# A macaron encoder block on one core: second-half FFN operands summed from PSUM, three pairs of products up front, filler transposes, and a new order in the mixer

## The chip, the cores and the metric

The kernel runs on one core of one Trainium2 chip. The metric is the device time of one execution in microseconds (us). Three runs of the kernel before gave 1774.66, 1774.74 and 1776.48 us, so the median is 1774.74 us.

## The reference

The reference computes one residual layer on a sequence of 1024 tokens with 1024 features, in float32:

```
x = x + 0.5 * swiglu(rmsnorm(x), w_gate, w_up, w_down)         # FFN 1, hidden width 2816
h = rmsnorm(x) @ w_in                                          # u 512 | v 512 | c_q 256 | c_kv 128 | k_rope 32
y_a = gelu(u) * (masked w_s[g] @ rmsnorm(gelu(v)) + b[g])      # 4 groups of 128 channels, blocks of 128 tokens
y_b = attention(q(c_q), k(c_kv, k_rope), v(c_kv))              # 8 heads, rmsnorm of q and k, rope, causal by chunks of 64
x = x + concat(rmsnorm(y_a), rmsnorm(y_b)) @ w_out
x = x + 0.5 * swiglu(rmsnorm(x), ...)                          # FFN 2
x = rmsnorm(x)
```

## The kernel before

**Products in two parts.** Every float32 operand of a matmul is split into a rounded high part (a cast on ACT) and a low part (a subtraction on DVE). Each product is then three matmuls on PE: high by high, high by low, low by high. One gate/up product of the FFN is 24 matmuls of 512 columns (line 464).

**Strassen in the FFN.** Each FFN multiplies by a seven-product scheme in place of eight. For each of 11 units of weight columns, `GateUp` makes seven products P1 to P7. P1 and P2 need only the first four row tiles of x (operands B11 and B21). P6, P5, P7, P3 and P4 need sums that contain the last four row tiles (T2, T1, T3, B22, T4). `XOps` makes these operands. `XOps.tile` (line 356) normalizes one row tile, transposes it on PE into two PSUM banks and copies both banks to SBUF on ACT. After the fourth tile it splits B11 and B21 from SBUF. For each of the last four tiles, `second` (line 371) forms T3, T2 and T4 from SBUF and splits T2. `rest` (line 392) forms T1 and splits the others later. The order of products begins with P1 and P2 of units 0 and 1 (`EARLY`, line 512). The PSUM group "a" of a unit, two of the eight banks, stays open from P1 to P4.

**The mixer.** Steps run in a list written out by hand (`for ch in ...`): u_t projects the gate channels of row tile t, m and g do the spatial mixing of a pair of tiles, a_t projects the latents, c_t transposes them and splits the result into `chl` (lines 290, 291), l_t (`latent_tile`, line 887) multiplies to queries, keys and values (lines 895 to 904), normalizes them and rotates the queries on POOL (lines 794 to 798). u4 to u7 stand between the latent steps. Attention follows after l7: 32 items, each of one head and a pair of row tiles. The first four items need only row tiles 0 to 3. `head_T` transposes the queries and keys of a head, four row tiles at a time; item 3 begins with those of row tiles 4 to 7.

**What sets the order.** A `Step` holds its work and work to be issued so many steps ahead (`before`). SBUF and PSUM places are planned from a dry run in which a matmul counts as one unit of time and any other operation as 0.01. A place whose earlier tile is still in use makes the later one wait. Small tiles rotate over 6 buffers for each width (line 179). Last, a scheduler that simulates the timeline puts the instructions of each engine in order, so that the order on an engine can differ from the order in the text. Loads go through SP's queue in program order.

Of the kernel before, what the change touches and what calls it, by code (L numbers as in the profile page):

```python
# [234 lines left out]
def block(nc, x, positions, ffn1_norm, ffn1_w_gate, ffn1_w_up,  # L235
# [61 lines left out]
    def transposed(src, name):  # L297
        halves = [bank(f"tp{i}_{name}") for i in range(2)]
# [51 lines left out]
    class XOps:  # L350
# [5 lines left out]
        def tile(self, i, xt, g):  # L356
            xn = tile_([P, D], f"xn{i}_{self.nm}")
            normed(xt, g, xn, f"{self.nm}{i}")
            hv = transposed(xn, f"{self.nm}{i}")
            n, c = i // 4, (i % 4) * P  # L360
            for k in range(2):
                if i % 4 == 0:
                    self.b[k, n] = tile_([P, 4, 512], f"b{k}{n}_{self.nm}")
                nc.scalar.copy(self.b[k, n][:, :, c:c + P], hv[k])
            if i == 3:
                self.split("B11", self.b[0, 0])
                self.split("B21", self.b[1, 0])
# [28 lines left out]
        def rest_of(self, key):  # L396
            b11, b12 = self.b[0, 0], self.b[0, 1]
            if key == "T1":
                for a, b in HALVES:
                    nc.vector.tensor_tensor(b12[:, a:b], b12[:, a:b], b11[:, a:b], op=ALU.subtract)  # L400
                    self.split("T1", b12, ((a, b),))
            else:
                self.split(key, {"T3": self.t3, "B22": self.b[1, 1], "T4": self.b[1, 0]}[key])
# [9 lines left out]
    class GateUp:  # L413
# [83 lines left out]
        def steps(self, order, floor=0, loaded=(), load_at=()):  # L497
            at = {}
            for u, (pn, ka, kb, pair) in order:
                st = at[u, pn] = Step(lambda u=u, a=(pn, ka, kb, pair): self.product(u, *a))  # L500
                if pn == "P1":
                    for k in range(2):
                        if (u, k) not in loaded:
                            lead = st.index - load_at[u] if u < len(load_at) else LEAD_LOAD - k
# [4 lines left out]
                st.before(LEAD_SPLIT, lambda u=u, ka=ka: self.split(u, ka), floor)  # L509
# [139 lines left out]
    xts = [row_tile(x[rows(0), :], "xa0")]  # L649
    g1 = row_tile(ffn1_norm[0].partition_broadcast(P), "g1")  # L650
    xts += [row_tile(x[rows(t), :], f"xa{t}") for t in (1, 2, 3)]
# [291 lines left out]
    vs = [Step(lambda t=t: v_tile(t)) for t in range(NT)]  # L943
    sm = {}
    works = {"u": u_tile, "m": mix_pair, "g": gmlp_pair, "a": latent_in, "k": key_rope, "c": latent_T, "l": latent_tile}
    for ch in ("u0 u1 m0 g0 u2 u3 m1 g1 a0 c0 a1 k0 l0 u4 c1 a2 l1 c2 a3 k1 l2 u5 m2 c3 a4 l3 g2 c4 a5 k2 l4 u6 "
               "c5 a6 c6 l5 a7 c7 k3 l6 u7 m3 l7").split():
        sm[ch] = Step(lambda f=works[ch[0]], n=int(ch[1]): f(n))
    v0 = vs[0].index
    vs[0].before(12, mix_gain)  # L950
    for t in range(4):
        steps[v0 - 5 + t].do(lambda t=t: mix_norm_tile(t))
    for t in range(4, NT):
        vs[t].before(4, lambda t=t: mix_norm_tile(t), v0)
    for j in range(2):
        vs[0].before(8 - j, lambda j=j: load_in("wv", j, GW, GW))
        sm["u0"].before(7 - j, lambda j=j: load_in("wu", j, 0, GW))
        sm["a0"].before(9 - j, lambda j=j: load_in("wa", j, 2 * GW, LAT))
    for k, (lv, lu, la) in enumerate(((4, 5, 7), (3, 5, 6), (2, 4, 5), (1, 3, 4))):
        vs[0].before(lv, lambda k=k: split_in("wv", k, GW))  # L960
        sm["u0"].before(lu, lambda k=k: split_in("wu", k, GW))
        sm["a0"].before(la, lambda k=k: split_in("wa", k, LAT))
    vs[0].before(3, v_gain)
    sm["u0"].before(3, spatial_weights)
    sm["u1"].before(0, out_gain)
    sm["a0"].before(6, load_uq)
    sm["a0"].before(4, latent_setup)
    sm["a0"].before(4, load_kv)
    sm["a0"].before(1, split_uq)
    sm["a0"].before(1, split_kv)  # L970
    sm["a0"].before(0, rope_tables)
    sm["l7"].do(lambda: mx.__setitem__("yB", [tile_([P, 4, H, DV], f"yB{i}") for i in range(2)]))

# [84 lines left out]
    for n in range(len(items) + D2):  # L1058
        st = att[n] = Step()
        if n == 0:  # L1060
            st.do(lambda: head_T(0, 0))
            st.do(lambda: head_T(1, 0))
        if n == 3:
# [16 lines left out]
    att[0].do(lambda: gmlp_pair(3))  # L1080
# [64 lines left out]
    gu2.steps(GU_ORDER, base2, load_at=(base2 - 1, base2))  # L1145
# [62 lines left out]
```

## Time and profile before

| | |
|---|---|
| median of 3 runs | 1774.74 us |
| profiled execution | 1775.43 us |
| its span, first to last instruction | 1773.4 us |
| PE busy | 1714.4 us (97%) |
| DVE busy | 1123.7 us (63%) |
| ACT busy | 757.0 us (43%) |
| mean granted TensorE clock | 0.989 |

PE is TensorE's matmuls, PEld its weight loads, DVE VectorE, ACT ScalarE, POOL GpSimd, SP the queue that issues loads. The granted clock is a share of full speed: 1.00 is 2.4 GHz and 0.50 is 1.2 GHz. An idle time is put down to the instruction that ended it, with an arrow.

### The profile page before, as it was taken

To read this page: it belongs to the slowest core of one execution; us is meant where nothing else is said; L and a number is where in the kernel's file an instruction comes from. 1 tells how busy PE (TensorE), PEld (TensorE's weight loads), DVE (VectorE), ACT (ScalarE), POOL (GpSimd) and SP (SyncE) were. 2 spreads that over 40 slices of the span, in tenths; PEclk is the share of its full clock that TensorE was granted. 3 is DMA by queue.
4 is the path that set the end of the run, shared out by engine and by line. 5 is a ranking of instruction groups with operands and counts; after the bars stand their busy time and mean duration, and the time that the engine had idled before them with its cause. 6 is when DMAs were issued, how large, how long until landed. Compare 5 with 4: busy or idle time off the path is not lost.

```text
span 1773.4 us, 21088 instructions
## 1 busy us (share of the span) xinstructions
PE 1714.4 (97%) x8132; PEld 1439.8 (81%) x8132; DVE 1123.7 (63%) x1497; ACT 757.0 (43%) x1151; POOL 149.5 (8%) x287
## 2 busy tenths in 40 slices
PE   7999999999999999988799999999999999999998
PEld 5788888888888888877699888778888888888886
DVE  7966556545578666554877644684656655558774
ACT  7523333334334444444777833352333233433442
POOL 2000000000000013322300511100000000000010
PEclk9999999999999999998899999999999999999999
DMA  6323232226844521200000332424233222683531
GB/s 202 115 93 119 98 111 89 96 89 220 311 129 162 183 85 48 69 10 3 13 1 1 120 101 87 140 95 137 76 120 108 95 90 90 231 301 110 179 129 48
DMA packets 122979, 199.48 MB, mean 112 GB/s; under 512 B 11008, under 2 KB 57600, under 8 KB 122880
## 3 DMA queue, kind: packets, MB, share of 16 engines
q1 hardware_dynamic: 118784, 184.52, 30.7%
q0 software_dynamic: 3520, 12.58, 1.8%
q8 instruction: 63, 1.03, 0.2%
q10 hardware_dynamic: 576, 1.05, 0.2%
q14 instruction: 36, 0.29, 0.0%
HBM read 143.07 MB, written 55.05 MB: 112 GB/s over the span
## 4 chain that ended last, share of the span: by engine, by line
PE 89%; DVE 4%; ACT 3%; DMA 1%; POOL 1%; issue 1%; SPq 0%; POOLq 0%; ACTq 0%; DVEq 0%
PE psum L464 45%; PE psum L594 8%; PE psum L596 8%; PE psum L597 8%; PE psum L1026 2%; PE psum L722 2%; PE psum L724 2%; PE psum L723 2%; PE psum L1125 1%; PE psum L1126 1%; PE psum L1128 1%; PE psum L300 1%; PE psum L1036 1%; PE psum L1035 1%; PE psum L997 1%
## 5 line engine op out<-in xcount | busy, mean ns | idle before, releaser
L480 DVE TENSOR_TENSOR P_b<-psum,P_b 128x1024 f32<-128x1024 f32 x33 | 40.3, 1222 | 93.0 <-PE psum L464 93.0
L480 DVE TENSOR_TENSOR P_a<-psum,P_a 128x1024 f32<-128x1024 f32 x33 | 40.3, 1222 | 91.8 <-PE psum L464 91.8
L470 ACT COPY P_b<-psum 128x1024 f32<-128x1024 f32 x33 | 33.4, 1014 | 70.3 <-PE psum L464 68.3
L470 ACT COPY P_a<-psum 128x1024 f32<-128x1024 f32 x33 | 33.4, 1013 | 69.1 <-PE psum L464 69.1
L271 POOL TENSOR_TENSOR r_fin<-ms_fin,mhalf 128x1 f32<-128x1 f32 x8 | 8.0, 1009 | 609.4 <-DVE ms_fin L269 609.3
L291 DVE TENSOR_TENSOR pl<-psum,ph 128x512 fp32r<-128x512 f32 (+1 forms) x80 | 48.5, 630 | 10.8 <-ACT ph L290 10.2
L481 ACT ACTIVATE P_a<-P_a 128x512 f32<-128x512 f32 x33 | 20.8, 631 | 80.8 <-DVE P_a L480 80.7
L1001 DVE TENSOR_REDUCE nm<-psum 128x1 f32<-128x128 f32 (+3 forms) x64 | 46.8, 749 | 11.8 <-PE psum L999 11.5
L481 ACT ACTIVATE P_b<-P_b 128x512 f32<-128x512 f32 x33 | 20.8, 632 | 73.0 <-DVE P_b L480 72.9
L1125 PE MATMUL psum<-woh,yh 128*128 128x512 f32 x128 | 50.5, 396 | 0.0
L1003 ACT ACTIVATE p<-psum,nm 128x128 f32<-128x128 f32 (+3 forms) x64 | 47.7, 750 | 6.4 <-DVE nm L1001 3.4
L1126 PE MATMUL psum<-wol,yh 128*128 128x512 f32 x128 | 50.2, 392 | 0.0
L703 POOL DMA_DIRECT2D x1d<-x_a x8 | 4.6, 580 | 510.6 <-DVE x_a L608 510.5
L1026 PE MATMUL psum<-ident,p 128*128 128x128 f32 x288 | 43.4, 281 | 3.8 <-ACT p L1003 3.8
L1128 PE MATMUL psum<-woh,yl 128*128 128x512 f32 x128 | 44.9, 391 | 0.0
L290 ACT CAST ph<-psum 128x512 fp32r<-128x512 f32 (+1 forms) x80 | 41.7, 559 | 7.0 <-PE psum L1026 6.8
L1036 PE MATMUL psum<-pl,vv 128*128 128x256 f32 x160 | 42.7, 293 | 1.2 <-DVE pl L291 1.2
L1035 PE MATMUL psum<-ph,vv 128*128 128x256 f32 x160 | 43.3, 294 | 0.2 <-ACT ph L290 0.2
L997 PE MATMUL psum<-kh,qh 128*128 128x512 f32 (+2 forms) x96 | 38.6, 404 | 1.0 <-ACT kh L986 0.9
L1026 PEld LDWEIGHTS psum<-ident,p 128*128 128x128 f32 x288 | 34.0, 145 | 6.4 <-ACT p L1003 4.8
L608 DVE SCALAR_TENSOR_TENSOR x_b<-psum,x_b 128x512 f32<-128x512 f32 x32 | 21.0, 686 | 26.9 <-PE psum L597 26.9
L464 PE MATMUL psum<-xB11h_f,A11h_a 128*128 128x512 f32 x88 | 35.4, 405 | 2.6 <-ACT xB11h_f L389 2.6
(525 smaller groups left out, 5753.3 us busy)
## 6 DMA issues: line engine op xcount, KB each, us to landing
raw_a<-in_ffn_w_gate SPq DMA_DIRECT2D x22, 512.0 KB, 4.3
raw_a<-in_ffn_w_up SPq DMA_DIRECT2D x22, 512.0 KB, 5.4
hd<-hS_a SPq DMA_DIRECT2D x44, 256.0 KB, 2.2
raw_b<-in_ffn_w_gate SPq DMA_DIRECT2D x22, 512.0 KB, 4.2
raw_b<-in_ffn_w_up SPq DMA_DIRECT2D x22, 512.0 KB, 5.2
hd<-hS_b SPq DMA_DIRECT2D x44, 256.0 KB, 2.1
aS_a<-hd SPq DMA_DIRECT2D x20, 512.0 KB, 4.2
wB_a<-in_ffn_w_down SPq DMA_DIRECT2D x20, 512.0 KB, 5.6
```

Source lines behind the costliest of these rows:

```text
L464: mm(o, lhs[:, 4 * m + k, :], rhs[:, k, :], start=pn in FIRST and n == 0, stop=n == 11, skip_group_check=True)
L470: nc.scalar.copy(ev[u, pn], bk)
L480: nc.vector.tensor_tensor(c, bk, c, op=ALU.add)
L594: mm(banks[t], hh[:, j, tl], dh[:, j, :], start=pn in DOWN_FIRST and c == 0 and j == 0, stop=False, skip_group_check=True)
L596: mm(banks[t], hh[:, j, tl], dl[:, j, :], start=False, stop=False, skip_group_check=True)
L597: mm(banks[t], hl[:, j, tl], dh[:, j, :], start=False, stop=c == 5, skip_group_check=True)
L1026: nc.tensor.transpose(ps[:, i * P:(i + 1) * P], prs[j][:, c * P:(c + 1) * P], ident)
L1035: mm(acc[:, 0:256], mx["vv"][c][:, h, :], hi, start=i == 0, stop=False)
L1036: mm(acc[:, 0:256], mx["vv"][c][:, h, :], lo, start=False, stop=i == len(pts) - 1)
L1125: mm(pe[e], yh[:, k, :], wh[:, es], start=k == 0, stop=False)
L1126: mm(pe[e], yh[:, k, :], wl[:, es], start=False, stop=False)
L1128: mm(pe[e], yl[:, k, :], wh[:, e * 512:(e + 1) * 512], start=False, stop=k == KD - 1)
```

## The change

1. `XOps.tile` splits B11 and B21 of the first four row tiles straight from PSUM, tile by tile (`cut`), and copies the plain values to SBUF as well (`keep`). In FFN 1 the `keep` copies and the B21 parts come after the fourth tile.
2. `second` takes T1 and T2 from PSUM in two subtractions. The two sums for T3 and T4 move to `rest`.
3. `EARLY` has P1 and P2 of three units. The `rest` steps and one row tile move back to fit.
4. In FFN 1 the first four tiles get their eight PSUM banks by name, the second row tile is loaded before the gain, and transposes of the identity matrix are issued ahead of the first tile (40) and after tiles 0, 1 and 2 (8 each). They are written to a bank that tile 3 overwrites.
5. In FFN 2 the first weights are loaded one step earlier, three units' weights are asked for at the head, and the splits may come one step earlier.
6. The mixer's order has all u, m and g steps before the latents, and attention items 0, 1 and 2 between the last latent steps. The attention functions move up in the file unchanged.
7. Small tiles rotate over 10 buffers.

```diff
-        self.smalls = ctx.enter_context(tc.tile_pool(name="sp", bufs=6))
+        self.smalls = ctx.enter_context(tc.tile_pool(name="sp", bufs=10))
...
-        def tile(self, i, xt, g):
+        def tile(self, i, xt, g, halves=None, later=False):
             xn = tile_([P, D], f"xn{i}_{self.nm}")
             normed(xt, g, xn, f"{self.nm}{i}")
-            hv = transposed(xn, f"{self.nm}{i}")
...
-                nc.scalar.copy(self.b[k, n][:, :, c:c + P], hv[k])
-            if i == 3:
-                self.split("B11", self.b[0, 0])
-                self.split("B21", self.b[1, 0])
+            hv = transposed(xn, f"{self.nm}{i}", halves)
...
+            work = [lambda key=key, v=v, op=op: op(key, v, cs) for key, v in zip(("B11", "B21"), hv) for op in (self.cut, self.keep)]
+            work.pop(0)()
+            return work if later else [w() for w in work]
+
+        def cut(self, key, v, cs):
+            hi, lo = (o[:, :, cs] for o in self.ops[key])
+            split(v, hi, lo)
+
+        def keep(self, key, v, cs):
+            nc.scalar.copy(self.b[key][:, :, cs], v)
...
-            nc.vector.tensor_tensor(t3, b22, b12, op=ALU.subtract)
-            nc.vector.tensor_tensor(t2, t3, b11, op=ALU.add)
+            nc.vector.tensor_tensor(t1, hv[0], b11, op=ALU.subtract)
+            nc.vector.tensor_tensor(t2, hv[1], t1, op=ALU.subtract)
             self.last = (nc.scalar.copy(hi, t2), nc.vector.tensor_tensor(lo, t2, f(hi), op=ALU.subtract))
-            nc.vector.tensor_tensor(b21, b21, t2, op=ALU.subtract)
+            nc.scalar.copy(b22, hv[1])
...
+            for a, e in HALVES:
+                if key == "T3":
+                    nc.vector.tensor_tensor(b["B21"][:, a:e], b["B21"][:, a:e], b["T2"][:, a:e], op=ALU.subtract)
+                    nc.vector.tensor_tensor(b["T2"][:, a:e], b["T2"][:, a:e], b["B11"][:, a:e], op=ALU.subtract)
+                self.split(key, b[{"T3": "T2", "T4": "B21"}.get(key, key)], ((a, e),))
...
-    EARLY = [(0, BY_NAME["P1"]), (0, BY_NAME["P2"]), (1, BY_NAME["P1"]), (1, BY_NAME["P2"])]
+    EARLY = [(u, BY_NAME[p]) for u in range(3) for p in ("P1", "P2")]
...
+    def warm(count):
+
+        for _ in range(count):
+            nc.tensor.transpose(tbanks[3, 1][:, 0:P], ident, ident)
+
+    warm(40)
+    later = []
     for t in range(4):
-        xo1.tile(t, xts[t], g1)
+        later.append(xo1.tile(t, xts[t], g1, [tbanks[t, k] for k in range(2)], True))
+        if t < 3:
+            warm(8)
+        if t == 1:
+            later[0].pop(0)(), later[1].pop(0)()
+    for work in (later[2].pop(0), later[3].pop(0), *(w.pop(0) for w in later), *(w.pop(0) for w in later)):
+        work()
...
-    for i, j in ((4, 0), (5, 0), (6, 1), (7, 1)):
+    for i, j in ((4, 0), (5, 0), (6, 1), (7, 2)):
...
-        for key, j in (("T1", 2), ("T3", 3), ("B22", 3), ("T4", 4)):
+        for key, j in (("T1", 4), ("T3", 5), ("B22", 5), ("T4", 6)):
...
-    for ch in ("u0 u1 m0 g0 u2 u3 m1 g1 a0 c0 a1 k0 l0 u4 c1 a2 l1 c2 a3 k1 l2 u5 m2 c3 a4 l3 g2 c4 a5 k2 l4 u6 "
-               "c5 a6 c6 l5 a7 c7 k3 l6 u7 m3 l7").split():
+    for ch in ("u0 u1 m0 g0 u2 u3 m1 g1 u4 u5 m2 g2 u6 u7 m3 g3 a0 c0 a1 k0 l0 c1 a2 l1 c2 a3 k1 l2 c3 a4 l3 c4 a5 k2 l4 "
+               "c5 a6 c6 a7 l5 c7 k3 x0 l6 x1 l7 x2").split():
+        if ch[0] == "x":
+            attend(int(ch[1]))
+            continue
...
-    gu2.steps(GU_ORDER, base2, load_at=(base2 - 1, base2))
+    gu2.steps(GU_ORDER, base2 - 1, load_at={(0, 0): base2 - 2, (0, 1): base2 - 1, (1, 0): base2, (1, 1): base2,
+                                             (2, 0): base2, (2, 1): base2})
```

## Rows read from the trace of the kernel before

**Rows 1.** The page, its first part (busy time of each engine, share of the span, instructions) and two lines of its second (busy tenths of PE and the granted clock in 40 equal slices of 44.3 us).

```profile
PE 1714.4 (97%) x8132; PEld 1439.8 (81%) x8132; DVE 1123.7 (63%) x1497; ACT 757.0 (43%) x1151; POOL 149.5 (8%) x287
...
PE   7999999999999999988799999999999999999998
...
PEclk9999999999999999998899999999999999999999
```

**Rows 2.** Busy time in stretches: the stretch and its length, then the busy us and instructions of PE, PEld, DVE, ACT and POOL, the granted clock, the share of the DMA engines and GB/s.

```profile
0.00:60.00 60.00, 46.00 (x203) 37.04 (x204) 48.22 (x59) 44.90 (x63) 11.35 (x23) 0.94 0.47 158
626.50:738.00 111.50, 111.50 (x544) 94.32 (x543) 73.88 (x112) 46.78 (x76) 29.53 (x33) 1.00 0.23 75
738.00:872.00 134.00, 108.69 (x505) 94.69 (x504) 75.00 (x213) 69.29 (x167) 47.26 (x98) 0.90 0.03 11
872.00:1025.00 153.00, 147.79 (x1086) 137.72 (x1085) 116.71 (x229) 118.39 (x275) 32.28 (x77) 0.99 0.12 41
1117.00:1165.00 48.00, 41.76 (x192) 33.27 (x191) 35.99 (x40) 25.54 (x33) 4.24 (x4) 1.00 0.41 136
...
0.00:19.40 19.40, 7.26 (x33) 5.83 (x33) 9.55 (x13) 12.98 (x21) 3.69 (x17) 1.00 0.91 326
19.40:26.40 7.00, 6.12 (x14) 4.40 (x15) 6.56 (x7) 5.88 (x8) 2.53 (x1) 0.52 1.07 357
```

**Rows 3.** Waits in 738 to 872 us, of PE (first two) and of ACT: who waited for whom, us in total, times, the longest.

```profile
PE psum L895 <- ACT chl L290: 9.9, 5, 3.9
PE psum L902 <- ACT chl L290: 1.0, 1, 1.0
ACT chl L290 <- POOL qn L798: 14.7, 4, 5.5
```

**Rows 4.** The timeline of POOL, ACT and PE around the second latent tile: start, duration, engine, line, operation.

```profile
762.91 0.73 POOL L798 TENSOR_TENSOR qn<-rt 128x256 f32<-128x256 f32 x1
783.09 0.73 POOL L798 TENSOR_TENSOR qn<-rt 128x256 f32<-128x256 f32 x1
763.68 0.48 ACT L290 CAST chl<-psum 128x384 fp32r<-128x384 f32 x1 [0.94 <-POOL qn L798]
774.92 1.28 ACT L852 ACT_TABLE_LOAD   x1
776.84 1.28 ACT L277 ACT_TABLE_LOAD   x1
783.86 0.48 ACT L290 CAST chl<-psum 128x384 fp32r<-128x384 f32 x1 [5.51 <-POOL qn L798]
769.92 0.81 PE L904 MATMUL psum<-wkv_h,chl 128*128 128x512 f32 x2
```

**Rows 5.** Groups by line in 738 to 872 us that are not of the latents: count, busy us and mean ns, idle before.

```profile
L277 ACT ACT_TABLE_LOAD x5 | 6.4, 1283 | 0.1
L852 ACT ACT_TABLE_LOAD x4 | 5.1, 1283 | 0.1
L874 DVE SCALAR_TENSOR_TENSOR ya<-u,r_ya,goA 128x512 f32<-128x512 f32 x5 | 4.3, 853 | 0.7 <-POOL r_ya L271 0.7
L868 DVE SCALAR_TENSOR_TENSOR u<-psum,bT,u 128x256 f32<-128x256 f32 x8 | 3.6, 479 | 6.5 <-PE psum L861 5.2 <-ACT u L852 1.2
L1001 DVE TENSOR_REDUCE nm<-psum 128x1 f32<-128x128 f32 (+3 forms) x6 | 2.2, 421 | 0.0
L987 DVE SCALAR_TENSOR_TENSOR kl<-psum,gkcol,kh 128x512 fp32r<-128x512 f32 x3 | 2.2, 736 | 0.0
```

**Rows 6.** The timeline of PE in the latent projection at full clock: two matmuls that stand three apart.

```profile
755.00 0.35 PE L722 MATMUL psum<-wa_h,xmh 128*128 128x416 f32 x1
755.56 0.35 PE L722 MATMUL psum<-wa_h,xmh 128*128 128x416 f32 x1
```

**Rows 7.** The head of FFN 1: waits of PE, then the timeline.

```profile
PE psum L464 <- ACT xB11h_f L389: 2.6, 1, 2.6
PE psum L464 <- DVE xB11l_f L390: 0.9, 1, 0.9
PE psum L464 <- DVE xT1l_f L390: 1.0, 1, 1.0
7.93 1.06 ACT L286 ACTIVATE xn_f<-xa 128x1024 f32<-128x1024 f32 x1 [2.16 <-DMA xa<-in_x]
14.09 1.28 DVE L305 SCALAR_TENSOR_TENSOR xn_f<-xa,r_f,g 128x1024 f32<-128x1024 f32 x1 [0.73 <-POOL r_f L271]
16.79 1.22 DVE L435 TENSOR_TENSOR S_a<-raw_a,raw_a 128x1024 f32<-128x1024 f32 x1 [0.28 <-PE psum L300]
18.26 2.00 ACT L389 CAST xB11h_f<-b_f 128x1024 fp32r<-128x1024 f32 x2
19.37 1.22 PE L464 MATMUL psum<-xB11h_f,A11h_a 128*128 128x512 f32 x2 [2.62 <-ACT xB11h_f L389]
```

**Rows 8.** Weight loads of the row tiles' transposes in FFN 1: the first tile (8 to 11 us) and the fourth (15.4 to 17 us) as groups, and the fifth, at about 30 us, from the timeline.

```profile
L300 PEld LDWEIGHTS psum<-ident,xn_f 128*128 128x128 f32 x8 | 1.6, 224 | 8.0 <-DVE xn_f L305 8.0
L300 PEld LDWEIGHTS psum<-ident,xn_f 128*128 128x128 f32 x8 | 1.1, 172 | 0.5 <-DVE xn_f L305 0.5
30.17 1.03 PEld L300 LDWEIGHTS psum<-ident,xn_f 128*128 128x128 f32 x8
```

**Rows 9.** The head of FFN 2: waits of PE in 1117 to 1165 us, and of SP's queue in 1085 to 1140 us.

```profile
PE psum L464 <- DVE S2l_b L450: 2.2, 1, 2.2
PE psum L464 <- DVE xT1l_f L390: 2.1, 1, 2.1
PE psum L464 <- ACT b_f L364: 1.3, 1, 1.3
SPq L311 <- PE psum L1128: 34.4, 4, 20.0
```

More of the change, by code (lines that the diff above doesn't have):

```diff
@@ L295, in split_scaled, with transposed @@
         nc.vector.scalar_tensor_tensor(lo, src, scale, f(hi), op0=ALU.mult, op1=ALU.subtract)
-    def transposed(src, name):
-        halves = [bank(f"tp{i}_{name}") for i in range(2)]
+    def transposed(src, name, halves=None):
+        halves = halves or [bank(f"tp{i}_{name}") for i in range(2)]
         for k in range(KD):
@@ L371, in second @@
-        def second(self, i, cs):
-            b11, b12, b21, b22 = (v[:, :, cs] for v in (self.b[0, 0], self.b[0, 1], self.b[1, 0], self.b[1, 1]))
+            hv = transposed(xn, f"{self.nm}{i}", halves)
+            cs = slice((i % 4) * P, (i % 4) * P + P)
+            if i >= 4:
+                return self.second(i, hv, cs)
+            if i == 0:
+                for k, key in enumerate(("B11", "B21")):
+                    self.ops[key] = [tile_([P, 4, 512], f"x{key}{n}_{self.nm}", F32R) for n in "hl"]
+                    self.b[key] = tile_([P, 4, 512], f"b{k}_{self.nm}")
@@ L396, in rest_of @@
         def rest_of(self, key):
[L397 to L403, printed above, removed]
+            b = self.b
+            for a, e in HALVES:
[3 more added lines that the diff above has]
+                self.split(key, b[{"T3": "T2", "T4": "B21"}.get(key, key)], ((a, e),))
     PRODUCTS = (("P1", "A11", "B11", "a"), ("P2", "A12", "B21", "b"), ("P6", "S2", "T2", "a"), ("P5", "S1", "T1", "c"),
@@ L495, in hsum, with steps @@
             nc.vector.tensor_tensor(t, self.h[u, x0], self.h[u, x1], op=op)
-        def steps(self, order, floor=0, loaded=(), load_at=()):
+        def steps(self, order, floor=0, loaded=(), load_at={}):
             at = {}
@@ L508, in steps @@
                         st.before(LEAD_SUM - which, lambda u=u, w=which: self.sums(u, w), floor)
[L509 removed]
+                st.before(LEAD_SPLIT if len(at) != 2 else 1, lambda u=u, ka=ka: self.split(u, ka), floor)
             return at
[L512 removed]
+    EARLY = [(u, BY_NAME[p]) for u in range(3) for p in ("P1", "P2")]
     GU_ORDER = EARLY + [(u, p) for u in range(NU) for p in PRODUCTS if (u, p) not in EARLY]
@@ L648, in block @@
     gu1 = GateUp("a", xo1, ffn1_w_gate[0], ffn1_w_up[0], hds[0])
-    xts = [row_tile(x[rows(0), :], "xa0")]
+    xts = [row_tile(x[rows(t), :], f"xa{t}") for t in range(2)]
     g1 = row_tile(ffn1_norm[0].partition_broadcast(P), "g1")
-    xts += [row_tile(x[rows(t), :], f"xa{t}") for t in (1, 2, 3)]
+    xts += [row_tile(x[rows(t), :], f"xa{t}") for t in (2, 3)]
     for k in range(2):
@@ L1057, in block, with attend @@
     att = {}
-    for n in range(len(items) + D2):
+    def attend(n):
         st = att[n] = Step()
@@ L1062, in block @@
             st.do(lambda: head_T(1, 0))
+        if n == D2 - 1:
+            st.do(lambda: mx.__setitem__("yB", [tile_([P, 4, H, DV], f"yB{i}") for i in range(2)]))
         if n == 3:
@@ L1078, in block @@
                 st.do(lambda i=items[n - D1]: weighted(*i))
-    att[0].do(lambda: gmlp_pair(3))
+    vs = [Step(lambda t=t: v_tile(t)) for t in range(NT)]
+    sm = {}
+    works = {"u": u_tile, "m": mix_pair, "g": gmlp_pair, "a": latent_in, "k": key_rope, "c": latent_T, "l": latent_tile}
+    for ch in ("u0 u1 m0 g0 u2 u3 m1 g1 u4 u5 m2 g2 u6 u7 m3 g3 a0 c0 a1 k0 l0 c1 a2 l1 c2 a3 k1 l2 c3 a4 l3 c4 a5 k2 l4 "
[3 more added lines that the diff above has]
+            continue
+        sm[ch] = Step(lambda f=works[ch[0]], n=int(ch[1]): f(n))
+    v0 = vs[0].index
+    vs[0].before(12, mix_gain)
+    for t in range(4):
+        steps[v0 - 5 + t].do(lambda t=t: mix_norm_tile(t))
+    for t in range(4, NT):
+        vs[t].before(4, lambda t=t: mix_norm_tile(t), v0)
+    for j in range(2):
+        vs[0].before(8 - j, lambda j=j: load_in("wv", j, GW, GW))
+        sm["u0"].before(7 - j, lambda j=j: load_in("wu", j, 0, GW))
+        sm["a0"].before(9 - j, lambda j=j: load_in("wa", j, 2 * GW, LAT))
+    for k, (lv, lu, la) in enumerate(((4, 5, 7), (3, 5, 6), (2, 4, 5), (1, 3, 4))):
+        vs[0].before(lv, lambda k=k: split_in("wv", k, GW))
+        sm["u0"].before(lu, lambda k=k: split_in("wu", k, GW))
+        sm["a0"].before(la, lambda k=k: split_in("wa", k, LAT))
+    vs[0].before(3, v_gain)
+    sm["u0"].before(3, spatial_weights)
+    sm["u1"].before(0, out_gain)
+    sm["a0"].before(6, load_uq)
+    sm["a0"].before(4, latent_setup)
+    sm["a0"].before(4, load_kv)
+    sm["a0"].before(1, split_uq)
+    sm["a0"].before(1, split_kv)
+    sm["a0"].before(0, rope_tables)
+    for n in range(3, len(items) + D2):
+        attend(n)
     wov = w_out[0].rearrange("(k p) e -> p k e", p=P)
```

46 lines of the change are left out of this document (9 added, 37 removed).

## The prediction

> **What bounds the kernel now.** I read the page first. PE is busy 97% of the span, and its line of tenths is full but for the first slice and for slices 18 to 20, where the granted clock dips too [rows 1]. So the kernel is bound by TensorE, no matmul is removed by the change, and all that can be won is time in which PE is idle or runs at 1.2 GHz. The table of stretches says where that is [rows 2]. From 626 to 738 us, the first half of the mixer, PE has no idle time. From 738 to 872 us, the latents, it is idle 134.0 - 108.7 = 25.3 us, and the mean clock is 0.90. In the head of FFN 1 it is idle 14.0 us of 60, in the head of FFN 2 6.2 us of 48. Attention (872 to 1025) loses 5.2 us, which the change leaves alone. Then I asked what PE waited for in each: in the latents mostly for `chl`, the latents' split on ACT, and that in turn for POOL's rotation of the tile before [rows 3].
>
> **The change part by part.**
>
> *Mixer.* First what it costs now. A mean of 0.90 over 134 us means that 10%, 13.4 us, of PE's rate was not granted. Some of this fell on idle time (25.3 of 134, a fifth), so I take 11 us as lost. With the idle time the stretch has 36 us above PE's own work.
>
> Where it comes from: in the timeline POOL ends a query at 763.64 and ACT begins `chl` at 763.68; POOL ends the next at 783.82 and ACT begins at 783.86 [rows 4]. That is a buffer that has to come free (the code has no other tie between them): the dry run counts a vector operation as nothing, and at this point weights for u, the gated unit's v, and the growing queries and keys share SBUF. Each such loop empties PE for several us and its clock falls. The four u steps inside make it worse on ACT: nine table loads of 1.28 us, 11.5 us, between Gelu and Sqrt [rows 5].
>
> After the change, u4 to u7 and the last two mixing pairs are done before the latents. Their PE work is moved and not removed. The u weights and v are dead by then, which frees over 12,000 floats per partition of a plan of some 51,000 (line 210), and the nine table loads fall to about four (one Sqrt after the last Gelu, and Exp against Sqrt at the end). So I expect the buffer loop to be gone. What then bounds a latent tile? PE: three matmuls of 416 columns take 0.56 us [rows 6], so a projection of 24 takes 4.5 us; the l step has 12 matmuls of 384 and 6 of 512 columns, 7680 columns against 9984, so 3.5 us; with the transposes 8.4 us. DVE: 75.0 us in the stretch, less 7.9 for the gated unit and some 7 for attention's first items [rows 2, 5], is 60 us, 7.5 a tile. POOL and ACT are below that. PE is the slowest, but only just: I leave 3 us for places where DVE's order holds it up. The tail is worse. From the last matmul of an l step (769.92, two matmuls, so about 770.6) to the end of its rotation (783.82) it was 13.2 us, of which two table loads are 2.6 [rows 4]. With one Exp against Sqrt load I take 12 us; item 2 of attention covers some 2.5, so 9.5 us of idle time before `head_T` of tiles 4 to 7, and 2.5 us of lower clock behind it. Sum left: 3 + 9.5 + 2.5 = 15 of the 36. **Mixer: -21 us**, between -30 (the tail is covered too) and +27 (second rival).
>
> *Head of FFN 1.* The first product now starts at 19.37 [rows 7]: the fourth tile is normalized at 14.09 + 1.28, transposed, copied on ACT, then cast from SBUF, with a weight sum in front on DVE. After the change the cast reads PSUM: 15.4, plus half a tile's transposes (0.55), plus a cast of 512 columns (half of 1.0, rounded up to 0.6) gives 16.5, so -2.9. The second row tile lands 1.3 us or so earlier by the swap of loads, which gives slack ahead of the fourth tile and no more. The wait for the low part (0.9) goes, since it is made per tile. So does the wait for T1 (1.0): three pairs of 2 x 5.3 us stand ahead of P6, one pair more than now, and DVE's sums per second-half tile fall from four to three. The two that are put off into `rest`, and unit 2's splits, come to some 7 us of DVE within those 10.7. Against it, B21's casts and the `keep` copies now stand on ACT behind the fourth tile, 16 casts and copies of about 0.6 in place of 8 copies and 4 casts of 1.0: I charge 1.0 us at the start of P2.
>
> The clock: from 19.4 to 26.4 it is 0.52 [rows 2], after PE stood idle 2.6 us. At half pace 7 us do the work of 3.5, and the change can win about 3.0 of it if the filler keeps the clock up. Whether a transpose can: the first tile's eight loads took 1.6 us and the fourth's 1.1, against 1.03 for a tile at full clock [rows 8], while nothing but transposes had run. So the pace did rise on transposes alone. (The clock column reads 1.00 up to 19.4 us, also where the pace was slow; in this stretch I go by the pace.) The filler has room: 40 at 0.2 us fill 8 us from 1.9 us on, and the fourth tile's transposes are not due until 15.4. **FFN 1: -2.9 - 0.9 - 1.0 - 3.0 + 1.0 = -6.8 us**, between -8 and +2 (third rival).
>
> The Trainium skill says otherwise of the filler: its page "TensorE: Matmul & The Clock Gate", section "Part 4: PE-mode transpose", says that a transpose does not count as activity for the clock. The pace of the fourth tile speaks against it in this kernel; by the page the filler would lift nothing, which is the third rival below.
>
> *Head of FFN 2.* Idle 6.2 us: 2.2 and 2.1 on DVE (S2's and T1's low parts), the rest on weights and banks at the first products [rows 9]. The third pair takes the first two away as above. The earlier load helps only if SBUF is free then, since SP's queue stood 34.4 us waiting for the output projection's matmuls [rows 9]. I keep 2.2 of the 6.2. **FFN 2: -4 us**, between -6 and +2 (six loads of 1 MB compete in place of four).
>
> *At nothing:* the ten small buffers (they free latent tiles' scalars; counted with the buffer loop); attention's functions moved in the file; u and g steps in front, where PE is never idle and DVE is 66% busy [rows 2]. If that cover were too thin, a pair of g steps on DVE would show as waits there.
>
> **Sum.** 1775.4 (the profiled execution) - 21 - 6.8 - 4 = 1743.6. The median of the runs stands 0.7 below the profiled one, so **1743 us**.
>
> **The rivals.**
>
> 1. *The buffer loop stays in half of the tiles.* For it: the plan's clock still ignores vector work. Against: over 12,000 floats are freed. The mixer then wins about 4 us, and the sum is 1775.4 - 4 - 10.8 - 0.7 = 1760.
> 2. *Slower: the loop stays in every latent tile, with no u steps left to fill it.* A loop took 783.86 - 763.68 = 20.2 us [rows 4]; without two table loads, 17.6. PE has 8.4 us of work in it, so it idles and stays at the lower clock. Eight loops of 17 are 136 us, and the moved u and m steps cost 25 us of PE before (four u of 5.5, two pairs of 1.4): 161 in place of 134, +27. With both heads' 10.8 won: 1791 us. It decides once a loop is longer than (134 - 25 + 10.8) / 8 = 15 us.
> 3. *The filler does not lift the clock.* 64 fillers and 24 transposes ahead of the fourth tile at 0.196 us are 17.3 us from 1.9, so its transposes start at 19.2 and the first product at 20.6 (half a tile at that pace, and the cast), 1.2 later than now, and the clock is low behind it. FFN 1 then gives +1.2 - 1.9 + 1.0 = +0.3 and the sum is 1750.
> 4. *Three open pairs fill PSUM.* Three groups "a" take six banks and P2's group the last two, so the third P2 waits for the second's evacuation and the row tiles' transposes wait too. Some 2.5 us in each head: 1748.
> 5. *The tail is covered as well*, because the scheduler pulls attention's work forward: mixer -30, 1734.
>
> **How the numbers follow.** Forecast 0.47, rival 1 0.20, rival 2 0.12 (with other slower ways 0.13), rival 3 0.06, rival 4 0.05, rival 5 0.09. What this kernel's times can tell from no change is 0.2%, 3.5 us. All but rival 2, and a tail of rival 1 that ends within 3.5 us of 1774.7 (0.05), are faster: 0.82 faster, 0.05 same, 0.13 slower. The range leaves out the slower cases and the fringe of the fifth: 1729 to 1768 us.
>
> **What would show it.** Right: waits of `chl` on POOL gone in the latents, table loads there four or five, PE idle there about 12 us, first product of FFN 1 at 16 to 17 us with the clock at 1.00, no wait for a T1 in either head. Wrong: `chl` still released by POOL at 15 us intervals or more; a first product later than 18 us; the clock near 0.5 after it; waits of line 464 for PSUM evacuation at the sixth product. A result over 1768 would mean that the mixer was misread, since the heads hold only 20 us in all.

## The result, and the profile after

The changed kernel takes 1761.19 us (median of 4 runs, 1760.48 to 1762.48) beside 1775.08 us before (a fourth run, 1775.41, moved the median of the kernel before by 0.3): a ratio of 0.9921, with an interval of 0.9904 to 0.9938. It is 13.9 us faster, where I forecast 32. The range held the time; the sum did not.

The page of the changed kernel, the lines that answer to [rows 1]:

```profile
PE 1715.3 (97%) x8196; PEld 1443.1 (82%) x8196; DVE 1123.5 (64%) x1501; ACT 748.3 (43%) x1147; POOL 142.0 (8%) x287
...
PE   8999999999999999999799999999999999999988
...
PEclk9999999999999999999899999999999999999999
```

Of the dip in slices 18 to 20 one slice is left, and a dip in slice 39 (1672 to 1716 us) is new. To see what each part gave I cut both traces at four matmuls that both have: the last of FFN 1 (its low part `aA22l`), the last of the mixer's fold, the last of the output projection, and the span's end. (The start of that matmul counts.) In us:

| stage | before | after | moved | forecast |
|---|---|---|---|---|
| FFN 1 | 660.4 | 664.7 | +4.3 | -6.8 |
| mixer | 373.6 | 352.4 | -21.2 | -21 |
| output projection | 94.0 | 93.0 | -1.0 | 0 |
| FFN 2 | 645.4 | 650.4 | +5.0 | -4 |
| span | 1773.4 | 1760.5 | -12.9 | -31.8 |

So the mixer did what was forecast, and both FFNs, which were to gain, lost. Stretches of the changed kernel, columns as in [rows 2]: the first 60 us, the first product alone, the latents as a whole, their tail, FFN 2's head, and a place late in FFN 2:

```profile
0.00:60.00 60.00, 52.24 (x263) 43.78 (x264) 45.27 (x61) 35.48 (x55) 7.80 (x41) 0.94 0.59 193
...
18.90:25.00 6.10, 6.04 (x14) 4.54 (x15) 4.36 (x7) 5.47 (x11) 0.85 (x2) 0.50 1.07 367
...
757.00:862.00 105.00, 90.97 (x495) 83.25 (x494) 76.87 (x220) 67.38 (x174) 40.58 (x86) 0.93 0.02 9
...
820.00:862.00 42.00, 28.94 (x160) 24.10 (x160) 33.18 (x78) 31.05 (x67) 14.74 (x34) 0.84 0.00 1
...
1100.00:1148.00 48.00, 44.54 (x205) 36.87 (x204) 32.29 (x34) 22.71 (x28) 2.27 (x4) 1.00 0.41 139
...
1680.00:1720.00 40.00, 35.47 (x147) 28.60 (x146) 23.59 (x29) 14.38 (x19) 5.34 (x8) 0.91 0.34 119
```

In the first row PE looks busier than before (46.0), but the filler counts as busy there. And the waits of PE in the changed kernel, in the same order (FFN 1's first 130 us, latents, FFN 2's head, late FFN 2), the last line being ACT's there:

```profile
PE psum L470 <- DVE bT_f L386: 2.7, 2, 1.4
PE psum L470 <- ACT xB11h_f L290: 2.1, 1, 2.1
...
PE psum L470 <- ACT A22h_a L455: 1.2, 1, 1.2
...
PE psum L470 <- ACT P_a L476: 0.9, 1, 0.9
...
PE psum L974 <- DVE kn L957: 6.1, 2, 3.4
PE psum L974 <- POOL qn L821: 2.9, 2, 1.5
...
PE psum L470 <- ACT A11h_b L455: 3.5, 1, 3.5
PE psum L470 <- ACT P_b L476: 1.1, 1, 1.1
...
PE psum L600 <- ACT wT3h_b L582: 4.5, 1, 4.5
...
ACT aS3h_b L573 <- DMA out<-o: 3.8, 1, 3.8
```

Gone are the waits for T1 and S2 [rows 7, 9] and, in the latents, `chl` waiting for POOL [rows 3]. PE's idle time there is 14.0 us, 13.1 of it in the tail, where the last keys' scaling on DVE (6.1) and the last queries' rotation on POOL (2.9) are awaited. The new ones have three causes, and the experiments take them one by one: a first product that is late all the same, the third pair, and a stored output tile near 1702 us that no part of the change touches.

### The profile page after: what moved, and what is told of

It reads as the page before. It is cut to its first block, busy times and chain, and to the rows that moved or that the text cites. A ratio compares the mean times of both kernels' runs of the same rounds, so it can differ in the third digit from the quotient of the medians.

```text
span 1760.5 us, 21191 instructions
## 1 busy us (share of the span) xinstructions
PE 1715.3 (97%) x8196; PEld 1443.1 (82%) x8196; DVE 1123.5 (64%) x1501; ACT 748.3 (43%) x1147; POOL 142.0 (8%) x287
## 4 chain that ended last, share of the span: by engine, by line
PE 90%; DVE 3%; ACT 3%; DMA 2%; issue 1%; POOL 1%; SPq 0%; POOLq 0%; ACTq 0%; DVEq 0%
PE psum L470 46%; PE psum L603 7%; PE psum L600 7%; PE psum L602 7%; PE psum L745 2%; PE psum L746 2%; PE psum L747 2%; PE psum L1154 2%; PE psum L1157 2%; PE psum L1155 2%; PE psum L1018 2%; PE psum L300 1%; PE psum L1028 1%; PE psum L1027 1%; PE psum L989 1%
## 5 line engine op out<-in xcount | busy, mean ns | idle before, releaser
L486 DVE TENSOR_TENSOR P_b<-psum,P_b 128x1024 f32<-128x1024 f32 x33 | 40.4, 1223 | 75.4 <-PE psum L470 75.4
L291 DVE TENSOR_TENSOR pl<-psum,ph 128x512 fp32r<-128x512 f32 (+1 forms) x80 | 48.6, 630 | 14.7 <-ACT ph L290 14.5
```

Of the source, the lines that this page charges most:

```text
L486: nc.vector.tensor_tensor(c, bk, c, op=ALU.add)
```

## The experiments

Every run is given with its ratio to the kernel before and the interval, and with the four stages in the order of the table (us, from its own trace).

### The parts alone

**e1**, the mixer's order alone on the kernel before (with attention's functions moved up as it needs):

```diff
-    for ch in ("u0 u1 m0 g0 u2 u3 m1 g1 a0 c0 a1 k0 l0 u4 c1 a2 l1 c2 a3 k1 l2 u5 m2 c3 a4 l3 g2 c4 a5 k2 l4 u6 "
-               "c5 a6 c6 l5 a7 c7 k3 l6 u7 m3 l7").split():
+    for ch in ("u0 u1 m0 g0 u2 u3 m1 g1 u4 u5 m2 g2 u6 u7 m3 g3 a0 c0 a1 k0 l0 c1 a2 l1 c2 a3 k1 l2 c3 a4 l3 c4 a5 k2 l4 "
+               "c5 a6 c6 a7 l5 c7 k3 x0 l6 x1 l7 x2").split():
...
```

> The kernel before with the reordered mixer alone (chunk order, first three attention steps in the chain; the six small buffers and both FFN heads as before). Theory (the mixer gave all of the gain and more, the heads took some back): about 1754 us, 21 below before, with no latent weight copy waiting on POOL in 738 to 872 us. Rival (the ten small buffers are what broke the buffer loop): 1765 or more, with the copies' waits on POOL still there. Rival (the mixer's 21 hang on the new heads through the plan of SBUF places): anywhere above 1760.

1751.37 us, 0.9865 (0.985 to 0.988): 660.3, 357.7, 93.1, 638.9. The order alone is worth 23 us, more than the whole change, and the ten small buffers have no part in it. In the latents no wait of ACT's `chl` on POOL is left. But 6.5 of the 23 lie in FFN 2, whose code is unchanged: PE's waits there fall to one line.

```profile
PE psum L464 <- DVE xT1l_f L390: 0.8, 1, 0.8
```

**e2**, the opposite: the changed kernel with the old order string.

> The changed kernel with the chunk order of the mixer put back as it was; both new heads and the ten small buffers stay. Theory: slower than before, 1777 to 1783 us: FFN 1 ends 4 us later, the FFN 2 head gains 2, and up to 7 more if the late wait of FFN 2 for the place of an output tile belongs to the heads. Rival (the heads do gain as forecast, and what the whole lost comes from the mixer's new order): 1764 to 1770.

1795.15 us, 1.0115 (1.0098 to 1.0132): 663.0, 385.9, 94.5, 651.7. The theory's 1783 was too low: both FFNs lost about what it said (2.6 and 6.3 against before), but 12 us more were lost in the mixer, whose order is the old one: 385.9 in place of 373.6. The waits in 755 to 885 us, first PE, then ACT, show the loop of [rows 3] grown, PE's part from 9.9 to 20.2 and POOL's from 14.7 to 19.6:

```profile
PE psum L918 <- ACT chl L290: 20.2, 4, 8.5
...
ACT chl L290 <- POOL qn L821: 19.6, 4, 5.5
```

**e3** and **e4**, the changed kernel with the whole head of one FFN as before: old `XOps`, two pairs, and the old times of its loads and splits; in e3 no filler, named banks or earlier second row tile either:

```diff
-    xo1 = XOps("f1")
+    xo1 = XOpsOld("f1")
...
-    xo2 = XOps("f2")
+    xo2 = XOpsOld("f2")
...
```

> The changed kernel with FFN 1's head as before (row copies, sums from SBUF, two pairs up front, no filler); the new mixer, the new FFN 2 head and the ten buffers stay. Theory (FFN 1's new head costs 4 us): about 1757 us, the last matmul of FFN 1 at about 660 us. Rival (the 4 us come from somewhere else, for instance from the place that each tile gets in SBUF): 1760 to 1762.

> The changed kernel with FFN 2's head as before; the new FFN 1 head, the new mixer and the ten buffers stay. Theory (its head gained 2 us, and the 7 us lost near 1702 us are an accident of the places in SBUF): 1763 if the wait near 1702 us stays, 1756 if it goes. Rival (the new head is itself a loss through later products): 1754 to 1756 with FFN 2 shorter before 1690 us.

e3: 1766.23 us, 0.9957 (0.9944 to 0.9969): 661.1, 359.2, 94.6, 651.1. e4: 1749.52 us, 0.986 (0.9846 to 0.9873): 663.1, 353.0, 93.1, 638.8. e3 is above both its expectations: FFN 1 ends near 660 as the theory said, but the mixer takes 6.8 us more, so the whole is 5 us slower than the changed kernel. e4 is below both of its own. FFN 2 decides: with the new head it takes 650 to 652 us in every run so far, with the old one in the new order 639. So its new head costs 11.6 us, where I still believed from comparing it with before that it gained 2. FFN 1's new head costs 2 to 4 us in FFN 1 (the five traces with this code, the changed kernel, e2, e4, e8 and e9, end it at 663.0 to 664.7, so differences of 1.7 there mean little), and with it the mixer is 5 to 7 us shorter (352 to 353 against 358 to 359), so that it gains in sum.

### The late wait in FFN 2

**e8** keeps the place of four stored tiles longer in the dry run:

```diff
-                    v.buf[2] = max(v.buf[2], d.clock + (HOLD if name == "dma_start" else 0.0))
+                    v.buf[2] = max(v.buf[2], d.clock + ((80.0 if v.buf[3] in ("o0", "o1", "o2", "o3") else HOLD) if name == "dma_start" else 0.0))
```

> The changed kernel with the place of each of the first four stored output tiles kept for 80 matmuls after its store in the plan of SBUF instead of 24; nothing else is edited (the plan of other tiles may shift). Theory (the wait near 1702 us is the place of a stored tile given out too soon): the wait of ScalarE's cast for the store is gone, the last down products begin 6 to 7 us earlier, 1754 us. Rival (ScalarE is late there for another reason, and only its last wait bears the store's name): the stall of 4 us stays at the same product, 1760 us or more.

1755.82 us, 0.9896 (0.9881 to 0.9911): 664.0, 353.2, 93.0, 644.6. The same stretch as above now has PE busy throughout at full clock:

```profile
1680.00:1720.00 40.00, 40.00 (x178) 33.13 (x177) 28.50 (x36) 19.77 (x29) 6.08 (x8) 1.00 0.33 119
```

The products on `wT3h_b` go from first to last start in 29.7 us in place of 36.8, so the stall cost 7.1. A place was kept for 24 matmuls, 24 x 0.228 = 5.5 us, and a store of an output tile took up to 8.5 us, as the view of that tensor in the changed kernel says:

```profile
DMA to landing us min/median/max: 2.0/2.5/8.5
```

The store of 8.5 us began at 1693.9. ACT's cast of S3 waited 3.8 us for it, to 1702.45, and PE 4.5; the granted clock of 1700 to 1710 us is 0.72 in the mean.

### The third pair in FFN 2

**e9** is e8 with two pairs up front in FFN 2, and with the old times of loads, splits and `rest` that go with them; the new operands stay:

```diff
-    gu2.steps(GU_ORDER, base2 - 1, load_at={(0, 0): base2 - 2, (0, 1): base2 - 1, (1, 0): base2, (1, 1): base2,
-                                             (2, 0): base2, (2, 1): base2})
-    rest(xo2, base2)
+    gu2.steps(GU_ORDER2, base2, load_at={(u, k): base2 - 1 + u for u in range(2) for k in range(2)})
+    for key, j in (("T1", 2), ("T3", 3), ("B22", 3), ("T4", 4)):
+        steps[base2 + j].do(lambda key=key: xo2.rest(key))
...
```

> The kernel of the run with the stored tiles' places kept longer (1755.8 us), with two pairs of products up front in FFN 2 instead of three; the new operands stay in both FFNs. Theory (FFN 2's head lost its 4.5 us to the third pair, whose weights come off the queue last): the waits of 3.5 and 1.1 us go, first to last split of FFN 2's gate and up as in the run with FFN 2's old head, about 1751 us. Rival (the operands summed from PSUM are what costs): waits on the subtractions or on T1 and T2 of 2 to 4 us in their place, 1755 us or more.

1751.01 us, 0.9872 (0.9851 to 0.9893): 663.5, 352.2, 94.6, 639.1. PE has no wait at all in 1098 to 1223 us. The 5.5 us in FFN 2 against e8 belong to the third pair together with its loads, which no run took apart. Its weights are the last of six loads: in the changed kernel the last transfer lands 14.4 us after the output projection's last matmul begins, in e9 1.2 after it. ACT's cast waits for that transfer, as its timeline says:

```profile
1124.64 1.04 ACT L455 CAST A11h_b<-raw_b 128x1024 fp32r<-128x1024 f32 x1 [2.91 <-DMA raw_b<-in_ffn_w_up]
```

PE's wait for that cast was 3.5 us, and the one for a bank, P1's copy, 1.1.

### The head of FFN 1

Why the first product is late shows in ACT's timeline in the changed kernel; PE's transposes of the fourth tile come first here, and PE's first product is the result:

```profile
15.77 1.09 PE L300 MATMUL psum<-ident,xn_f 128*128 128x128 f32 x8 [0.75 <-DVE xn_f L305]
...
15.86 0.60 ACT L376 COPY b_f<-psum 128x512 f32<-128x512 f32 x1
16.34 0.61 ACT L290 CAST xB11h_f<-psum 128x512 fp32r<-128x512 f32 x1
16.82 0.62 ACT L376 COPY b_f<-psum 128x512 f32<-128x512 f32 x1
17.30 0.63 ACT L290 CAST xB21h_f<-psum 128x512 fp32r<-128x512 f32 x1
17.77 0.64 ACT L376 COPY b_f<-psum 128x512 f32<-128x512 f32 x1
18.25 0.65 ACT L290 CAST xB11h_f<-psum 128x512 fp32r<-128x512 f32 x1
...
18.96 1.22 PE L470 MATMUL psum<-xB11h_f,A11h_a 128*128 128x512 f32 x2 [2.10 <-ACT xB11h_f L290]
```

In the code the B21 casts stand behind the fourth tile, and so do the `keep` copies but for two, which item 1 of the change left out: B11's of tiles 0 and 1 are issued after tile 1. On ACT four copies and three B21 casts came ahead of that tile's B11 cast, the last line of ACT above, so the scheduler moved two copies and three casts forward. ACT is never idle here: half the tile is transposed at about 16.3 us, and the cast begins at 18.25, a queue's length late. **e6** ties the copies and B21's casts behind it (`nc.after` makes them wait for that cast):

```diff
...
+    with nc.after(cast):
-    for work in (later[2].pop(0), later[3].pop(0), *(w.pop(0) for w in later), *(w.pop(0) for w in later)):
-        work()
+        for work in (later[2].pop(0), later[3].pop(0), *(w.pop(0) for w in later), *(w.pop(0) for w in later)):
+            work()
```

> The changed kernel with the plain copies of the row tiles and the remaining casts issued only after tile 3's first cast. Theory (ScalarE's order, casts and plain copies of tiles 0 to 2 ahead of tile 3's cast, makes the first product late and lets the clock fall): first product at 17 to 17.5 us, the clock in 20 to 40 us above the changed kernel's 0.88, FFN 1 ends 2 to 4 us before 664.7. Rival (a later wait takes it back, since the copies then come late for T1): first product at 17 to 17.5, FFN 1 ends where it did.

1759.52 us, 0.9916 (0.9901 to 0.9931): 659.3, 352.3, 94.6, 651.5. The fourth tile's transposes, ACT, PE and the stretch behind it in e6:

```profile
14.42 1.09 PE L300 MATMUL psum<-ident,xn_f 128*128 128x128 f32 x8 [0.37 <-DVE xn_f L305]
...
15.48 1.08 ACT L375 CAST xB11h_f<-psum 128x512 fp32r<-128x512 f32 x2
...
16.62 0.73 PE L474 MATMUL psum<-xB11h_f,A11h_a 128*128 128x512 f32 x2 [1.10 <-ACT xB11h_f L375]
...
16.50:24.50 8.00, 7.55 (x31) 5.60 (x32) 5.88 (x10) 8.00 (x17) 0.55 (x1) 1.00 1.05 377
```

The first product begins at 16.62 us, 2.3 sooner, the clock stays at 1.00, and FFN 1 ends 5.4 us sooner, more than the theory had. Not all of the 2.3 us are the tie's. From the fourth tile's first transpose to the first product it is 3.19 us in all seven traces with filler and without the tie, and 2.20 in the three with both and three pairs (e6, e11, e16): 1.0 us. Some 0.4 more come ahead of that: from ACT's first work on the fourth tile to its first transpose it is 4.4 to 4.5 us without the tie and 4.1 in those three. The other 0.9 us are a row tile's landing: ACT's first work on the third tile, which waits for that landing, begins at 8.98 in e6 and 9.90 in the changed kernel, and between 8.94 and 9.90 in the traces without the tie, whose loads are all the same. So a fairer measure of the tie is FFN 1's end in those runs: 659.1 to 659.8 with it, 663.0 to 664.7 without, about 4 us. That is what is left after a new wait of 3.4 us, from 31 us on. Of e6's 5.4 us 2.8 are left at the span's end and 1.7 in the median, since the output projection took 1.6 and FFN 2 1.1 us longer, both unedited.

**e5** leaves out the filler (all `warm` calls).

> The changed kernel without the identity transposes between the row tiles; all else stays. Theory (the first product waits for ScalarE's casts, not for TensorE's clock, so the filler buys little): the first product at 18.5 to 19.5 us as in the changed kernel, and FFN 1 ends within 1.5 us of the changed kernel's 664.7. Rival (the filler does hold the clock up for the row tiles): the row tiles' transposes take longer, the first product begins after 20 us, FFN 1 ends 3 us later or more.

1763.12 us, 0.9934 (0.9919 to 0.9949): 661.9, 353.0, 93.8, 649.3, first product at 18.49. FFN 1 ends 2.8 us sooner without the filler, which neither side had (1.1 to 2.8 against all five traces of FFN 1 as changed), and the median is within 2 us of the changed kernel's. The filler did lift the pace of the row tiles, as weight loads of transposes in the timeline show, first of the changed kernel (tile 0), then of e5 (tiles 0 and 1 together, then 2):

```profile
10.11 0.86 PEld L300 LDWEIGHTS psum<-ident,xn_f 128*128 128x128 f32 x8 [0.43 <-DVE xn_f L305]
```

```profile
9.85 3.27 PEld L300 LDWEIGHTS psum<-ident,xn_f 128*128 128x128 f32 x16 [9.85 <-DVE xn_f L305]
13.55 0.89 PEld L300 LDWEIGHTS psum<-ident,xn_f 128*128 128x128 f32 x8 [0.43 <-DVE ms_f L269]
```

Without it tiles 0 and 1 go at half the pace, but tile 3, the only one that is waited for, goes at the full one either way. The filler speeds up what is not late.

**e7** has two pairs in FFN 1 (`rest` at steps 2, 3, 3, 4, row tile 7 at step 1 and the weights' splits as before).

> The changed kernel with two pairs of products up front in FFN 1 as before instead of three, with the schedule of the row tiles and splits that went with them; the new operands and the filler stay, and FFN 2 is as changed. Theory (three open pairs leave too few PSUM banks and make the transposes of tiles 4 to 7 wait): the two waits of 1.4 us on the subtractions of the row tiles go, FFN 1 ends 2 to 3 us before 664.7. Rival (three pairs are what hides the operands' work): new waits for T1 or T2 of 2 us and more, FFN 1 ends later than 664.7.

1760.0 us, 0.9915 (0.9899 to 0.9932): 662.4, 354.0, 93.7, 649.0. The waits on L386 go, but others come, and the first product's is the same:

```profile
PE psum L470 <- DVE xB11l_f L291: 2.4, 1, 2.4
PE psum L470 <- ACT xB11h_f L290: 2.1, 1, 2.1
PE psum L470 <- DVE P_a L486: 1.9, 1, 1.9
```

FFN 1 ends 2.3 us sooner, as the theory said, but only 0.6 to 2.3 sooner than the five traces of FFN 1 as changed, and with new waits in place of the two that went. The third pair in FFN 1 is worth little either way.

### The parts together

**e11** is e4 with e6's tie; **e12** is the same without filler; **e16** has e6's tie, e8's places and e9's two pairs in FFN 2, so the new operands in both FFNs; **e17** is e16 with two pairs in FFN 1 too.

> The new mixer, FFN 1's new head with the plain copies behind tile 3's first cast, and FFN 2's head as before; no longer places. Theory (the parts add up, measured as: new heads of FFN 1 with old FFN 2 head 1749.5, minus 3 to 5 us for the first product): 1745 to 1747 us. Rival (the plan of places shifts a wait into the mixer or FFN 2): 1749 us or more, with one named wait of over 3 us that the run with FFN 2's old head doesn't have.

> The same without the identity transposes. Theory (the filler buys nothing, since the first product waits for ScalarE): within 1.5 us of the run with them. Rival (with the first product at 17 us TensorE itself is what is late, and the filler now counts): 2 to 4 us slower than with them, the row tiles' transposes longer than 1.1 us for eight.

> The new order, the new operands in both FFNs, three pairs in FFN 1 and two in FFN 2, the plain copies behind tile 3's first cast, the stored tiles' places kept for 80. Theory (the sums straight from PSUM are worth nothing on TensorE's path, they only move work): the same as the best run so far, 1746 to 1749 us. Rival (they are worth the two T1 waits of about 1 us each): 1744 to 1746. Rival (they load VectorE and cost): 1750 or more.

> As the run with the new operands in both FFNs (1747.7 us), with two pairs up front in FFN 1 too, and the schedule of row tiles and splits that went with them. Theory (the third pair costs in FFN 1 also, by the wait of 3.4 us at its start near 31 us and the full banks): FFN 1 ends 2 to 4 us before 659.8, the whole 1744 to 1746. Rival (the third pair does hide the operands' work): waits for T1, T2 or the sums of 3 us and more in its place, FFN 1 ends at 660 or later, 1748 or more.

| run | us | ratio (interval) | FFN 1 | mixer | out | FFN 2 |
|---|---|---|---|---|---|---|
| e11 | 1747.97 | 0.9855 (0.9837 to 0.9873) | 659.1 | 353.0 | 94.0 | 638.8 |
| e12 | 1751.21 | 0.9873 (0.9857 to 0.9889) | 661.5 | 355.2 | 94.0 | 638.8 |
| e16 | 1747.74 | 0.9852 (0.9838 to 0.9867) | 659.8 | 353.8 | 94.6 | 639.0 |
| e17 | 1749.81 | 0.9872 (0.9855 to 0.9888) | 659.3 | 354.9 | 94.5 | 639.0 |

e11 and e16 beat both kernels, by 26 us the one before and by 13 the changed one. e11 is 1 us above what was expected. e16 equals e11, as its theory had it: in FFN 2 the sums from PSUM are worth nothing in time (639.0 against 638.8; e16 also keeps e8's places). e12 was 3.2 us slower, as the rival had it, but not for its reason: its first product began at 16.47 with the clock at 1.00 to 24.4 us, so the filler was not missed there; PE's waits from 30 us on are 2 us longer, and the mixer, which was not edited, is 2.2 longer. Since e5 gained in FFN 1 without the filler and e12 lost, neither run shows that the filler itself is worth anything. e17's total fits the rival, its FFN 1 neither side: the 3.4 us at 31 us go, but the first product is held 2.3 us by DVE for a low part and the clock falls, so that FFN 1 ends only 0.5 us before e16's; 1.1 more are lost in the mixer, which was not edited.

```profile
16.50:24.50 8.00, 5.70 (x14) 4.21 (x15) 7.70 (x11) 7.60 (x14) 0.23 (x1) 0.60 1.05 377
```

### What the old order's loop depends on

**e10** is before with ten small buffers; **e13**, **e14** and **e15** are before, e2 and e1 with every place kept longer:

```diff
-HOLD = 24.0
+HOLD = 40.0
```

> The kernel before with ten small buffers instead of six, nothing else. Theory (the ten buffers change nothing by themselves, and the 12 us that the old chunk order lost more with the new heads come from the plan of places and the planner's order): 1774 us, within 0.3% of before. Rival (the ten buffers lengthen the latents by 12 us under the old order, through the smaller rest of SBUF or other waits): 1783 us or more. Rival (they break the buffer loop a little): 1768 or less.

> The kernel before with every place in SBUF kept for 40 matmuls after a transfer in the plan instead of 24; no instruction is changed. Theory (the old order's loop over the latents is as long as the plan of places makes it): the time from FFN 1's end to the mixer's last fold moves by 4 us or more either way from 373.6, and the whole time with it. Rival (the plan matters little, and the loop is the order's own): within 2 us of 373.6, the whole within 0.3% of before.

> The run with both new heads and the old order (1795 us), with places kept for 40 matmuls instead of 24. Theory (the 12 us more in the mixer are the plan's, and the late stall of FFN 2 too): the mixer's part falls from 385.9 to between 368 and 380, the late stall of 7 us is gone, the whole 1775 to 1785 us. Rival (the heads' own work, reaching into the mixer, makes the loop longer): the mixer's part stays at 384 or more.

> The run with the new order alone (1751.4 us), with places kept for 40 matmuls instead of 24. Theory (the new order has taken the loop away, so the plan now has little to act on): the mixer's part within 5 us of 357.7 and the whole 1746 to 1756 us. Rival (the plan acts as strongly as in the old order): more than 8 us either way.

| run | us | ratio (interval) | FFN 1 | mixer | out | FFN 2 |
|---|---|---|---|---|---|---|
| e10 | 1773.9 | 1.0 (0.9991 to 1.001) | 660.4 | 375.3 | 94.0 | 642.8 |
| e13 | 1774.84 | 1.0013 (1.0001 to 1.0024) | 663.2 | 374.9 | 94.5 | 639.7 |
| e14 | 1785.98 | 1.0071 (1.0056 to 1.0086) | 663.0 | 382.9 | 94.5 | 644.0 |
| e15 | 1755.39 | 0.9897 (0.9882 to 0.9912) | 662.5 | 356.2 | 94.3 | 639.6 |

The ten buffers do nothing under the old order. My theory of the places fell for the mixer: other places move it by 1 to 3 us (e13, e14, e15), not by 12 (e14, at 382.9, met neither side there), and POOL still holds `chl` for 14.7 us in e13, as in [rows 3]. What does differ is the order on the engines. Comparing the sequences of operations and tiles in the latents, PE's in e10 and e13 have 98% in common with before's, in e2 79%, though the text there is the same. That the scheduler's order makes the loop longer is thus likely, but no run set the one order in the other kernel, and it stays open; so does why the mixer is 5 to 7 us shorter with FFN 1's new head. In the FFNs, on the other hand, places do count. In FFN 1 they cost 2.8 us in e13 and 2.2 in e15 with no instruction changed (PE waits 2.2 us for T1 in place of 1.0), so part of the new head's 2 to 4 us could be places too; no run tells. In FFN 2 e13 takes 639.7 in place of 645.4, and of the 2.2 and 2.1 us in FFN 2's head [rows 9] 1.0 and 0.4 are left. In e14 the late stall is gone too.

## Why the prediction was right or wrong

*Mixer, -21: right in its mechanism, and by some luck in its number* (-21.2). The buffer loop is gone, and the tail has 13.1 us of idle time against 12 forecast, at a mean clock of 0.84, though most of the wait there is for the keys on DVE and not for the rotation. The table loads are six, not four. With the old heads the order alone gives -15.9 in the mixer (e1), so some 5 us of the agreement come from FFN 1's side, by a way that stays open.

*Head of FFN 1, -6.8: failed, +4.3.* The step that failed is "plus a cast of 512 columns (half of 1.0, rounded up to 0.6) gives 16.5". It has the cast begin as soon as half the tile is transposed, since I charged the `keep` copies and B21's casts to the start of P2, trusting the text's order. On ACT tile 2's cast, two copies and a B21 cast came first from the time that half was ready, so the cast began 2.0 us late and the first product at 18.96; the term of -2.9 became -0.4. That e6 begins at 16.62 is not the forecast come true: there the cast still waits 1.0 us behind another and a copy, and its tile came 1.0 us sooner than the 15.4 of the sum. With the first product's time fell the term of -3.0: the first 6.0 us of it ran at 0.50, a loss of 3.0 again (3.4 before). The waits for the low part and for T1 did go (-1.9), and 4.8 us of new waits came: 2.7 for banks that T1's and T2's subtractions hold on DVE, where the fourth rival had 2.5, and 2.1 on ACT. These terms come to +2.1; the other 2 us of the +4.3 lie in no listed wait, and their cause stays open.

*Head of FFN 2, -4: failed, +5.0.* Two steps. The first is "The third pair takes the first two away as above". The waits did fall, but an earlier landing of the weights does that with the old head: counted from the start of the output projection's last matmul, the last weights that two pairs need land at 7.1 us before the change, at 2.5 in e13 and at 2.8 in e1. And the third pair's own cost, 5.5 us with its loads (e8 against e9), was only a fringe of the range ("six loads of 1 MB compete in place of four"). The second is that the sum has no term for the late stall: every edit was priced where it stands in the text, but the plan of SBUF is one for the whole kernel. Of the 11.6 us that the new head costs beside the old one in the new order (e4), 5.5 are thus the third pair's and 5.8 the stall's (e8). The table shows only +5.0 since the new order by itself takes 6.5 off FFN 2 (e1), which the sum had not either.

*The rivals.* The third's FFN 1 (+0.3) is nearer than mine but 4 us off, and its reason is not the one: e5 and e12 show that the first product does not hang on the filler. The fourth was right in kind in FFN 1 (banks); in FFN 2 the bank is 1.1 us and the wait for weights, which it did not have, 3.5. The first's total (1760) was met by accident, as the loop had not stayed.

## What to carry to other kernels

When operands are made in pieces, look at what the producing engine does just before the piece that is waited for; a copy that only needs to be done "later" has to be tied there, since a scheduler will fill a gap with it. A plan of memory that counts transfers by a fixed time couples far parts: after any change, look for new waits on a store or load in stages that were not edited. And test the parts alone: here one part (e1) was worth 23 us and the whole 14.

## What the runs showed of the hardware

*Transposes and the clock.* In e5 nothing but transposes ran on TensorE up to the first product, as the weight loads shown with that run say; 16 weight loads took 3.27 us (0.204 each), the next eight 0.89 (0.111 each). With the filler in front even tile 0's eight took 0.86. So here transposes alone brought the pace up. The Trainium skill's page "TensorE: Matmul & The Clock Gate", section "Part 4: PE-mode transpose", says of transpose mode that the full clock doesn't engage for it, as it does not count as busy in the same way; for the float32 transposes of this trace the pace disagrees, and the measurement decides. The granted-clock column showed 1.00 all the while, so at the head of a kernel it is no guide to the pace.

*What came ahead of a fall.* In the changed kernel the clock fell to 0.50 at 18.1 us, during the 2.1 us of idle time ahead of the first product, and rose at 24.9; in e6 and e12, after 1.1 and 0.4 us, it stayed at 1.00 there; in e17, with 2.3 us idle inside the product, it fell. But in e5, with 1.3 us ahead of the product and 0.4 inside it, the clock also fell, 2 us into the product (0.50 from 20.5 to 23.9 us). And the same 2.1 us of idle time came with 6.8 us at 0.50 in the changed kernel, e4 and e8, but with 3.4 us in e2 and e9, from 19.3 on. So the length of one pause does not decide it alone. In the changed kernel the fall cost 3.0 us of PE's work, in e2 and e9 1.7, so 1.3 us of a difference between two such traces say nothing of their edits.
